# A decoder block on one core: a third split buffer in the input projection's seven products, a moved emptying of PSUM banks, a delayed multiply in the last norm

## The chip, the core and the metric

The kernel runs on one core of a Trainium2 chip. Its engines work side by side and wait for each other through semaphores: TensorE (PE in the profile, with its weight loads as PEld), VectorE (DVE), ScalarE (ACT), GpSimd (POOL) and SyncE (SP, which here issues the DMAs of the weights). The metric is the device time of one execution in microseconds, as the median of several runs. The chip's profiler also recorded one execution; from that record come the profile page and every view quoted here.

## What is computed

One layer for 256 positions of a model of width 2048, everything in float32:

```python
x = x + 0.5 * swiglu_ffn(rms_norm(x, ffn1_norm), w_gate1, w_up1, w_down1)   # d_ff = 5632
z = rms_norm(x, mix_norm) @ w_in                                           # 2048 -> 5 * 1024
lru_x, lru_gate, sc_b, sc_c, sc_x = split(z, 5)
xc = causal_depthwise_conv(lru_x, lru_conv_w) + lru_conv_b
y_lru = rg_lru(xc, ...) * gelu(lru_gate)
y_sc = sc_b * causal_depthwise_conv(sc_c * sc_x, sc_conv_w)
y = concat([rms_norm(y_lru, lru_out_norm), rms_norm(y_sc, sc_out_norm)])
x = x + y @ w_out
x = x + 0.5 * swiglu_ffn(rms_norm(x, ffn2_norm), w_gate2, w_up2, w_down2)
return rms_norm(x, final_norm)
```

The stages are called ffn1, the mixer (with the input projection `w_in`), the output projection, ffn2 and the final norm in what follows. In the code `D` is 2048, `S` is 256 positions, `NT` is 2 (tiles of 128 positions), `CW` is 512 (columns of one block), `UK` is 4 (rows of 128 in one unit).

## The kernel before

**Units of weight.** All weights pass through as units of 512 rows by 512 columns (1 MB, one DMA on SP's queue into the pool `raws`, or a larger buffer). Float32 accuracy comes from splitting: ACT casts a unit to a rounded high part (two casts of 128x1024), DVE subtracts it from the raw unit to get the low part (one operation of 128x2048), and PE multiplies high by high, high by low of the activations, and low by high. That is `parts_of` (L207) with `split_tiles` (L193) and `low_part` (L202). In a trace a unit is a pair `hi_...`, `lo_...`; a unit used for one target has 8 matmuls with the high part and 4 with the low part, each 128x512.

**Where the high and low parts lie.** `split_tiles` takes them from the pool `splits`, which has two buffers of each. While the list `extra` is not empty, every call counts `turn_of["split"]` up, and each third call takes its pair from the pool `extra[0]` instead, where that pair has one buffer. Both ffn stages put their own pool in `extra` (L523) and empty it at their end; the output projection does so with the pool `op` (L1250). Nothing resets the count. Pools on the same side of the memory that are opened one after the other use the same bytes: the pool of ffn2 is opened where `op` has been closed.

**The seven products.** `seven` (L411) multiplies two blocks of rows and columns with seven products in place of eight: p0, p4, p5, p6, p2, p3 and p1 on sums and differences of raw units made by DVE (rows `raw_x<-raw_x,raw_x`), and between them the units x01, x11, x00, x10, which are used as they are. Its banks of PSUM are called a, c, e and d; after p0 and p4 their contents are put aside as the snapshots s1 and s5 (later u2 and u3), and the bank is used again. A function `between`, if it is given, is called at fixed places: `between(0)` after s5, `between(1)` after x01, and so on. Ffn1 and ffn2 run `seven` for gate, up and down projections; the input projection runs it once, as in_c, inside `sc_c`; the output projection as o_q.

**The input projection.** `columns` (L332) computes four banks of 128 columns by 256 positions over four units. The first call (in_0_0) is followed by `use(ps, half)`, which is `lru_x` there: it empties the four banks with two copies by ACT and two adds and multiplies by DVE for each pair (rows `half_x` and `zx`), and then `sc_c()` runs the seven products in_c. The next call of `columns` is in_0_1.

**The output projection.** `product` o0 in two halves (g0, g1) inside the mixer, then, with the pool `op`, `product` o3 in two halves (units o3_0_0, o3_0_1, o3_1_2, o3_1_3) and the seven products o_q with their snapshots in `op`. The results are added into `xres`, the residual (rows `xres<-ps_...`, and `xres<-s_o_q` for the snapshot s1, the last of all). The norm for ffn2 needs squares of `xres` (`junk_n`) and its transposes (`pt_n`).

**Ffn2 and the end.** Ffn2 begins with the units g2_0_0, u2_0_0, g2_0_1, u2_0_1 and so on. Its last down projection is a `product` d2_9_0, the seven products d2_9, and a `product` d2_9_3. Each finished block c of 512 columns of `xres` goes through `last(c, t)` (L1302): a square with its sum on ACT, and on DVE a multiply of `xres` by -0.5 and by the final gain `fin`. `close` then scales the rows and writes them out.

**Who orders the work.** SP's DMAs keep the order of the program. For the other engines a scheduler orders the instructions when the kernel is built, from its own estimates of times and the dependences between tiles; on the chip each engine then runs its own list strictly in that order.

Of the kernel before, what the change touches and what calls it, by code (L numbers as in the profile page):

```python
# [49 lines left out]
def hybrid_block(ctx: ExitStack, tc: tile.TileContext, a: dict, out: bass.AP):  # L50
# [121 lines left out]
    def big(name):  # L172

        return bigs.tile([P, UK, 2 * S], F32R, tag="big", name=name)
# [4 lines left out]
    turn_of = {"split": 0}  # L179

    def load(src, name, pieces=((0, UK),), loaded=None, kept=False):
        if kept and extra:
            raw = extra[0].tile([P, UK, CW], F32, tag="kept", name=f"raw_{name}", bufs=2)
        elif kept:
            raw = bigs.tile([P, UK, CW], F32, tag="big", name=f"raw_{name}")
        else:
            raw = raws.tile([P, UK, CW], F32, tag="raw", name=f"raw_{name}")
        for i, e in pieces:
            sp.dma_start(raw[:, i:e, :], src[i * P : e * P].rearrange("(j p) c -> p j c", p=P))
            if loaded:  # L190
                loaded(i)
        return raw

    def split_tiles(name):
        pool, bufs = splits, 2
        if extra:
            turn_of["split"] += 1
            if turn_of["split"] % 3 == 0:
                pool, bufs = extra[0], 1
        return [pool.tile([P, UK, CW], F32R, tag=part, name=f"{part}_{name}", bufs=bufs) for part in ("hi", "lo")]  # L200

# [319 lines left out]
    def ffn(tag, norm, after, opening=False):  # L521
        with tc.tile_pool(name=f"ffn{tag}", bufs=1, side="left") as fp:
# [26 lines left out]
            def settle():  # L549
                while waiting:  # L550
                    turn_hidden(*waiting.pop(0))
# [312 lines left out]
            for s in range(5):  # L864
                cs = (CW + 2 * s * CW, 2 * CW + 2 * s * CW)
                sg = {}

                def total(ps, tiles):
                    for p in tiles[1:]:
                        dve.tensor_tensor(tiles[0], tiles[0], p, op=ALU.add)  # L870
                    if not tiles:
                        return ps
                    dve.tensor_tensor(tiles[0], ps, tiles[0], op=ALU.add)
                    return tiles[0]

                def gate(t, n, ps, tiles):
                    g = total(ps, tiles)
                    sg[t, n] = tiles[0] if tiles else keep(f"z{tag}_{s}")
                    act.activation(sg[t, n], g, AF.Silu)

                def up(t, n, ps, tiles):
                    dve.tensor_tensor(sg[t, n], total(ps, tiles), sg[t, n], op=ALU.mult)
                    if (t, n) == (1, 0):
                        settle()
                    waiting.append((1 + 2 * s + n, t, sg[t, n], s % 2 == 0))

                def meanwhile(i):
                    if opening and s == 0:
                        two, last, high, low = left[0]
                        if i == "first sum":  # L890
                            two()
                        elif i == "second product":
                            for k in (5, 6):
                                high(k)
                                low(k)
                        elif i == "third sum":
                            last()
                            high(2)
                        elif i == "third low":
                            low(2)  # L900
                        elif i == "fifth product":
                            Engine.pinned = False
                        elif i == "sixth product":
                            first_hidden()
                    elif i == 1:
                        settle()
                    elif s == 0 and i == 0:
                        sums()

                seven(wg, (0, 1), cs, sf, xs, f"g{tag}_{s}", keep, gate, meanwhile, opening and s == 0)  # L910
                sp.held = False
                seven(
                    wu, (0, 1), cs, sf, xs, f"u{tag}_{s}", keep, up,
                    (lambda i: settle() if i == 1 else None) if opening and s == 0 else None,
                )
                if s % 2 == 0:
                    down(s == 4)
# [49 lines left out]
    with tc.tile_pool(name="mixer", bufs=1, side="left") as mp, tc.tile_pool(name="mixw", bufs=2, side="left") as mw:  # L967
# [168 lines left out]
            last()  # L1136
            part(2)

        def sc_c():
            r2 = work.tile([P, NT], F32, tag="r2", name="r2")  # L1140
            dve.tensor_tensor(r2, nm.r, nm.r, op=ALU.mult)
            rt = [r2[:, t : t + 1] for t in range(NT)]
            room = [tmp(tag, "snap", 4 * S, bufs=1) for tag in "vd"]
            free = [b[:, o : o + CW] for b in room for o in (0, CW)]
            z = {}

            def turn(n):
                for f in range(0, 4, 2):
                    pt = bank(f"pt_c{n}_{f}")
                    for i in range(2):  # L1150
                        for t in range(NT):
                            o = i * S + t * P
                            pe.transpose(pt[:, o : o + P], z[t, n][:, (f + i) * P : (f + i + 1) * P], ident)
                    for i in range(2):
                        q = 4 * (1 - n) + f + i
                        c = tmp("cc", q, S + 2, bufs=8)
                        nc.gpsimd.memset(c[:, :2], 0.0)
                        act.copy(c[:, 2:], pt[:, i * S : (i + 1) * S])
                        cc[q] = c

            def done(t, n, ps, tiles):
                for p in tiles[1:]:
                    dve.tensor_tensor(tiles[0], tiles[0], p, op=ALU.add)
                    free.append(p)
                if tiles:
                    z[t, n] = tiles[0]
                    dve.scalar_tensor_tensor(z[t, n], ps, rt[t], z[t, n], op0=ALU.mult, op1=ALU.add)
                else:
                    z[t, n] = free.pop()
                    act.activation(z[t, n], ps, AF.Copy, scale=rt[t])  # L1170
                if (t, n) == (1, 0):
                    turn(1)

            c0 = 3 * (D // 2)
            seven(
                w_in, (0, 1), (c0 + CW, c0), si, [(u, nm.xT[u]) for u in (2, 3)], "in_c", lambda name: free.pop(0), done,
                factor={"s1": rt[0], "s5": rt[1], "u2": rt[0], "u3": rt[1]},
            )
            return lambda: turn(0)

        def sc_x(ps, half):
# [25 lines left out]
        for i, (use, part, half) in enumerate(order):  # L1207
            ps = columns(w_in, part * (D // 2) + half * CW, nm.xT, f"in_{part}_{half}", behind)
            behind = None
            if i == 0:  # L1210
                flush()
                nm.factor()
                nm.diagonals()
                nm.rows()
                bc = nm.bc
                use(ps, half)
                behind = sc_c()
                gate_weights("a", a["lru_w_a"][0])
                gate_weights("i", a["lru_w_i"][0])
                yT += [big(f"yT_{u}") for u in range(KD // UK)]  # L1220
            else:
                use(ps, half)
# [76 lines left out]

    fss = const.tile([P, NT, NC_D], F32, name="fss")  # L1300
    ov = out.rearrange("(t p) d -> p t d", p=P)

    def last(c, t):
        if c == 0 and t == 0:
            held["fin"] = bigs.tile([P, D], F32, tag="big", name="fin")
            nc.scalar.dma_start(held["fin"], a["final_norm"].partition_broadcast(P))
        fin = held["fin"]
        cs = slice(c * CW, (c + 1) * CW)
        xr = xres[:, t, cs]
        part = fss[:, t, c : c + 1]  # L1310
        junk = work.tile([P, CW], F32, tag="junk", name=f"junk_f_{c}_{t}", bufs=1)
        act.activation(junk, xr, AF.Square, accum_out=part)

        def single(tag):
            return work.tile([P, 1], F32, tag=tag, name=f"{tag}_{t}")


        dve.scalar_tensor_tensor(xr, xr, -0.5, fin[:, cs], op0=ALU.mult, op1=ALU.mult)
        if c == NC_D - 2:
            pre = held[t] = single("pre")  # L1320
            dve.reduce_sum(pre, fss[:, t, : c + 1], axis=AX.X)
            dve.tensor_scalar(pre, pre, 1.0 / D, EPS, op0=ALU.mult, op1=ALU.add)
            if t == 0:
                lastgain = fin[:, D - CW :]
                dve.tensor_scalar(lastgain, lastgain, -0.5, None, op0=ALU.mult)
            act.activation(single("root"), pre, AF.Sqrt)
# [66 lines left out]
```

## Time and profile before

| | us |
|---|---|
| median of 3 runs (lowest to highest) | 1729.67 (1729.08 to 1730.92) |
| profiled execution, its own time | 1729.74 |
| its span in the profile | 1728.0 |
| PE busy | 1716.6 |
| DVE busy | 1509.8 |
| ACT busy | 1077.7 |

How to read it: times in a timeline are microseconds from the start of the span. A row `947.87 0.16 DVE L43 COPY tot_y<-pst 128x2 f32<-128x2 f32 x1 [0.33 <-PE pst L43]` says that one copy (x1) from `pst` to `tot_y` began at 947.87 and took 0.16 us, and that DVE had stood still for 0.33 us before it, until PE had written `pst`. All operations pass through one helper, so they carry the same line, L43, and are told apart by the names of their tiles; numbers and indices at the end of a name are left out (`hi_in_c_p` is the high part of any of p0 to p6, `x8` at the end counts the operations of the group). Matmuls overlap, so the step from one group's start to the next group's start is a better measure of what a group takes than its own duration. A view of windows gives for each engine the busy time and, in brackets, the number of instructions, then the granted clock of PE, the share of the DMA engines and GB/s.

### The profile page before, as it was taken

How to read it: one execution, taken by the hardware profiler on the slowest of the kernel's cores; microseconds unless marked ns; L12 is line 12 of the kernel's file. 1: busy time of each engine (PE TensorE's matmuls, PEld its weight loads, DVE VectorE, ACT ScalarE, POOL GpSimd, SP SyncE). 2: the span in 40 equal slices, each digit the busy share in tenths (PEclk: the TensorE clock that was granted, in tenths of full speed). 3: DMA queues.
4: the chain of work that ended last, by engine and by line, in shares of the span. 5: the costliest groups of instructions: out<-in, count | busy, mean ns of one | idle time of the engine just before them, and what ended most of it. 6: DMA issues, size and time to landing. Idle time of an engine off the chain costs nothing.

```text
span 1728.0 us, 20332 instructions
## 1 busy us (share of the span) xinstructions
PE 1716.6 (99%) x7985; PEld 1433.5 (83%) x7985; DVE 1509.8 (87%) x1239; ACT 1077.7 (62%) x1406; POOL 7.0 (0%) x34
## 2 busy tenths in 40 slices
PE   9999999999999999999999999999999999999998
PEld 8888888888888888878888888888888888888886
DVE  7998989899789898787897989889899887899896
ACT  7666566656466666667966657656556664656654
POOL 0100000000000000000000000000000000000000
PEclk9999999999999999999999999999999999999999
DMA  8564565666466556555566574675665646555743
GB/s 300 191 237 141 208 228 186 206 230 219 156 211 204 202 178 219 171 169 197 172 195 203 188 243 144 199 240 187 212 210 195 218 147 219 195 195 195 257 156 122
DMA packets 174223, 343.22 MB, mean 199 GB/s; under 512 B 5684, under 2 KB 8624, under 8 KB 174000
## 3 DMA queue, kind: packets, MB, share of 16 engines
q1 hardware_dynamic: 173632, 340.81, 58.5%
q8 instruction: 62, 1.02, 0.2%
q10 hardware_dynamic: 176, 1.06, 0.2%
q14 instruction: 33, 0.27, 0.0%
q0 software_dynamic: 320, 0.07, 0.0%
HBM read 339.82 MB, written 2.10 MB: 198 GB/s over the span
## 4 chain that ended last, share of the span: by engine, by line
PE 97%; DVE 1%; DMA 1%; issue 0%; ACT 0%; DVEq 0%; ACTq 0%
PE ps_d L43 13%; PE ps_in L43 10%; PE ps_u_a L43 9%; PE ps_g_a L43 9%; PE ps_g_c L43 6%; PE ps_u_c L43 6%; PE ps_d_a L43 5%; PE ps_u_d L43 5%; PE ps_g_d L43 4%; PE ps_u_e L43 3%; PE ps_d_c L43 3%; PE ps_g_e L43 3%; PE ps_g L43 3%; PE ps_o L43 3%; PE ps_u L43 3%; PE ps_d_d L43 3%
## 5 line engine op out<-in xcount | busy, mean ns | idle before, releaser
L43 ACT CAST hi_g_p<-raw_g 128x1024 fp32r<-128x1024 f32 (+1 forms) x139 | 142.6, 1057 | 102.9 <-DVE raw_g L43 32.6
L43 DVE TENSOR_TENSOR lo_g_p<-raw_g,hi_g_p 128x2048 fp32r<-128x2048 f32 x70 | 159.7, 2287 | 32.0 <-ACT hi_g_p L43 31.8
L43 ACT CAST hi_u_p<-raw_u 128x1024 fp32r<-128x1024 f32 x140 | 141.4, 1050 | 67.6 <-DVE raw_u L43 24.7
L43 DVE TENSOR_TENSOR lo_u_p<-raw_u,hi_u_p 128x2048 fp32r<-128x2048 f32 x70 | 159.2, 2286 | 19.7 <-ACT hi_u_p L43 19.4
L43 PE MATMUL ps_d<-hi_d,h 128*128 128x512 f32 x696 | 166.1, 390 | 0.0
L43 PEld LDWEIGHTS ps_d<-hi_d,h 128*128 128x128 f32 x696 | 130.0, 188 | 26.7
L43 ACT CAST hi_d<-raw_d 128x1024 fp32r<-128x1024 f32 x88 | 88.6, 1048 | 71.6 <-PE ps_u_d L43 17.4
L43 DVE TENSOR_TENSOR lo_d<-raw_d,hi_d 128x2048 fp32r<-128x2048 f32 x44 | 100.6, 2290 | 31.8 <-ACT hi_d L43 31.8
L43 PE MATMUL ps_in<-xT_nm,hi_in 128*128 128x512 f32 x512 | 122.5, 391 | 0.0
L43 ACT CAST hi_d_p<-raw_d 128x1024 fp32r<-128x1024 f32 x84 | 85.1, 1050 | 59.3 <-DVE raw_d L43 40.2
L43 PEld LDWEIGHTS ps_in<-xT_nm,hi_in 128*128 128x128 f32 x512 | 94.0, 188 | 18.9 <-ACT tha L43 0.5
L43 ACT CAST hi_g_x<-raw_g 128x1024 fp32r<-128x1024 f32 (+1 forms) x79 | 81.5, 1059 | 41.7 <-PE ps_g_c L43 24.6
L43 ACT CAST hi_u_x<-raw_u 128x1024 fp32r<-128x1024 f32 x80 | 80.4, 1046 | 38.7 <-PE ps_u_c L43 22.1
L43 DVE TENSOR_TENSOR lo_d_p<-raw_d,hi_d_p 128x2048 fp32r<-128x2048 f32 x42 | 95.6, 2287 | 7.9 <-ACT hi_d_p L43 7.7
L43 DVE TENSOR_TENSOR raw_u<-raw_u,raw_u 128x2048 f32<-128x2048 f32 x40 | 91.6, 2290 | 10.9 <-DMA raw_u<-in_ffn_w_up_dram 10.2
L43 DVE TENSOR_TENSOR lo_g_x<-raw_g,hi_g_x 128x2048 fp32r<-128x2048 f32 x40 | 91.4, 2286 | 7.7 <-ACT hi_g_x L43 7.6
L43 DVE TENSOR_TENSOR lo_in<-raw_in,hi_in 128x2048 fp32r<-128x2048 f32 x32 | 73.3, 2289 | 25.3 <-ACT hi_in L43 25.2
L43 DVE TENSOR_TENSOR raw_g<-raw_g,raw_g 128x2048 f32<-128x2048 f32 x40 | 91.5, 2288 | 4.2 <-DMA raw_g<-in_ffn_w_gate_dram 3.7
L43 DVE TENSOR_TENSOR lo_u_x<-raw_u,hi_u_x 128x2048 fp32r<-128x2048 f32 x40 | 91.4, 2285 | 0.2 <-ACT hi_u_x L43 0.2
L43 PE MATMUL ps_d<-lo_d,h 128*128 128x512 f32 x348 | 86.2, 389 | 0.0
L43 ACT CAST hi_in<-raw_in 128x1024 fp32r<-128x1024 f32 x64 | 63.9, 1044 | 25.4 <-PE ps_in L43 13.8
L43 PEld LDWEIGHTS ps_d<-lo_d,h 128*128 128x128 f32 x348 | 65.3, 188 | 13.6
(471 smaller groups left out, 3740.9 us busy)
## 6 DMA issues: line engine op xcount, KB each, us to landing
raw_d<-in_ffn_w_down_dram SPq DMA_DIRECT2D x88, 1024.0 KB, 5.1
raw_u<-in_ffn_w_up_dram SPq DMA_DIRECT2D x87, 1024.0 KB, 5.3
raw_g<-in_ffn_w_gate_dram SPq DMA_DIRECT2D x86, 1024.0 KB, 5.3
raw_in<-in_w_in_dram SPq DMA_DIRECT2D x32, 1024.0 KB, 5.1
raw_in_c<-in_w_in_dram SPq DMA_DIRECT2D x8, 1024.0 KB, 5.1
raw_o<-in_w_out_dram SPq DMA_DIRECT2D x8, 1024.0 KB, 5.1
raw_o_q<-in_w_out_dram SPq DMA_DIRECT2D x8, 1024.0 KB, 5.1
xres<-in_x_dram SPq DMA_DIRECT2D x3, 512.0 KB, 10.0
```

The lines of the kernel that those rows point to most:

```text
L43: ins = getattr(self.engine, name)(*args, **kwargs)
```

## The change

It does four things.

1. In `sc_c`, `extra` holds the pool `bigs` (ten large buffers) while in_c runs, and is emptied after it. `split_tiles` then counts in_c's eleven splits, and each third one takes its high and low part as two of the large buffers. `load` is fitted to that: a unit that is to be kept goes to the same pool as before.
2. `sc_c` takes a function `between`. The emptying of the first columns' banks, `use(ps, half)`, is no longer called ahead of `sc_c` but inside it, at `between(1)` of in_c, after the unit x01.
3. In `last`, the multiply by the final gain is put in a list `gains` and done at the next call with c other than 0. For c = 0 (two operations) it comes later; for the others it is done at once, as before.
4. One line gets a space at its end.

```diff
     def load(src, name, pieces=((0, UK),), loaded=None, kept=False):
-        if kept and extra:
+        if kept and extra[0] is not bigs:
             raw = extra[0].tile([P, UK, CW], F32, tag="kept", name=f"raw_{name}", bufs=2)
...
             turn_of["split"] += 1
             if turn_of["split"] % 3 == 0:
+                if extra[0] is bigs:
+                    return [big(f"{part}_{name}") for part in ("hi", "lo")]
                 pool, bufs = extra[0], 1
...
-        def sc_c():
+        def sc_c(between):
...
             c0 = 3 * (D // 2)
+            extra.append(bigs)
             seven(
                 w_in, (0, 1), (c0 + CW, c0), si, [(u, nm.xT[u]) for u in (2, 3)], "in_c", lambda name: free.pop(0), done,
+                lambda i: between() if i == 1 else None,
                 factor={"s1": rt[0], "s5": rt[1], "u2": rt[0], "u3": rt[1]},
             )
+            extra.clear()
             return lambda: turn(0)
...
-                use(ps, half)
-                behind = sc_c()
+                behind = sc_c(lambda: use(ps, half))
...
+    gains = []
 
     def last(c, t):
...
-        dve.scalar_tensor_tensor(xr, xr, -0.5, fin[:, cs], op0=ALU.mult, op1=ALU.mult)
+        gains.append(lambda: dve.scalar_tensor_tensor(xr, xr, -0.5, fin[:, cs], op0=ALU.mult, op1=ALU.mult))
+        if c:
+            while gains:
+                gains.pop(0)()
```

## The prediction

> **What bounds the kernel now.** I read the page's first part, then its chain of work that ended last, then the waits of TensorE (PE), and only after these the timeline around each place that the change touches.
>
> ```profile
> span 1728.0 us, 20332 instructions
> ...
> PE 1716.6 (99%) x7985; PEld 1433.5 (83%) x7985; DVE 1509.8 (87%) x1239; ACT 1077.7 (62%) x1406; POOL 7.0 (0%) x34
> ...
> PE 97%; DVE 1%; DMA 1%; issue 0%; ACT 0%; DVEq 0%; ACTq 0%
> ```
>
> PE is busy for 1716.6 of 1728.0 us and is 97% of the chain: whatever doesn't make PE wait longer or less costs nothing. The profiled execution took 1729.74 us by its own time, 1.7 us beside the span and 0.07 above the median of the runs (1729.67), so sums made on it stand for the median. The waits say how little can be won:
>
> ```profile
> engine line waited for: us in total, times, longest us
> PE idle L43 <- DVE ones L43: 1.1, 1, 1.1
> PE ps_in_c_c L43 <- ACT v_snap L43: 0.8, 1, 0.8
> PE ps_u_c L43 <- DVE lo_u_p L43: 0.8, 1, 0.8
> PE ps_d_a L43 <- DVE lo_d_p L43: 0.3, 1, 0.3
> ```
>
> The first wait is the start of the run, the third stands in ffn1; the change touches neither. The second (the seven products named in_c) and the fourth (the last ones, in ffn2's last down projection) are its two targets.
>
> **In_c: the moved adds and the third buffer.** The block's opening in the timelines of PE, VectorE (DVE) and ScalarE (ACT), whose columns are start, time, engine, operation, count, and in brackets the wait before:
>
> ```profile
> 732.20 1.07 PE L43 MATMUL ps_in_c_a<-lo_in_c_p,xT_nm 128*128 128x512 f32 x4
> 733.11 1.98 PE L43 MATMUL ps_in_c_c<-hi_in_c_p,xis 128*128 128x512 f32 x8
> 734.92 1.98 PE L43 MATMUL ps_in_c_e<-hi_in_c_x,xT_nm 128*128 128x512 f32 x8
> 736.87 1.21 PE L43 MATMUL ps_in_c_c<-lo_in_c_p,xis 128*128 128x512 f32 x4
> 738.87 2.10 PE L43 MATMUL ps_in_c_c<-hi_in_c_x,xT_nm 128*128 128x512 f32 x8 [0.78 <-ACT v_snap L43]
> 731.87 0.75 DVE L43 TENSOR_TENSOR half_x<-ps_in,half_x 128x256 f32<-128x256 f32 x2
> 733.87 0.75 DVE L43 TENSOR_TENSOR zx<-half_x,bc_nm 128x256 f32<-128x256 f32 x2
> 734.53 2.28 DVE L43 TENSOR_TENSOR lo_in_c_p<-raw_in_c,hi_in_c_p 128x2048 fp32r<-128x2048 f32 x1
> 738.12 0.69 ACT L43 ACTIVATE v_snap<-ps_in_c_c,r 128x512 f32<-128x512 f32 x1 [1.62 <-PE ps_in_c_c L43]
> ```
>
> Four matmuls take 0.91 us undisturbed (732.20 to 733.11), eight 1.81 (733.11 to 734.92). From 734.92 on the steps are 1.95 for eight and 2.00 for four: 0.14 and 1.09 too long, 1.23 in all. The cause is readable: eight adds and multiplies of DVE (731.87 to 734.53, 2.66 us) stand ahead of the low part of unit p4, so the four low matmuls wait until 736.87, the snapshot of their bank until 738.12, and the next use of that bank until 738.87. In the order in which the built changed kernel issues DVE's work the eight stand behind that low part. Taking 2.66 from 734.53 gives 731.87; but the low part of x01, now in a buffer of its own, and one more sum have come ahead of it, and it is ready about 734.2 by my count, while PE wants it at 734.92. The bank's snapshot then falls near 736.4, its next use at 737.64: this stall goes. No instruction is added; the eight adds only go later, behind 2.28 us low parts that have about 0.2 us to spare where they are thinnest (the next pair). Against it, at the end of the block:
>
> ```profile
> 772.37 1.99 ACT L43 CAST hi_in<-raw_in 128x1024 fp32r<-128x1024 f32 x2 [0.61 <-DMA raw_in<-in_w_in_dram]
> 773.56 2.71 PE L43 MATMUL ps_in<-xT_nm,hi_in 128*128 128x512 f32 x11
> ```
>
> The next columns' first cast waits for its DMA, and PE starts 0.15 us after the first half of that cast (772.37 + 1.0 = 773.4). A PE that is 1.23 us earlier would stand there unless the load, issued by SP behind a buffer that DVE frees, also comes earlier; by the order it does, nearly as much. I give back some 0.1. In_c: **-1.1**, bounds -1.23 and -0.5.
>
> **The phase of the count.** The change also does something that it doesn't name. `turn_of["split"]` is one count for the whole kernel, and in_c now adds its 11 splits to it. 11 leaves 2 over 3, so from the output projection on, other units are the third ones. In the outs, unit o3_0_0 and o3_1_3 come from the large pool in place of o3_1_2; and ffn2's very first unit, g2_0_0, comes from the newly opened pool of ffn2, whose memory was the outs' own. Before, that unit took its turn in the ordinary buffers:
>
> ```profile
> 1013.82 2.00 ACT L43 CAST hi_g<-raw_g 128x1024 fp32r<-128x1024 f32 x2 [0.19 <-PE ps_o_q_a L43]
> 1020.84 2.28 DVE L43 TENSOR_TENSOR lo_u<-raw_u,hi_u 128x2048 fp32r<-128x2048 f32 x1
> 1023.03 0.74 DVE L43 SCALAR_TENSOR_TENSOR xres<-ps_o_q_a,r_y,xres 128x512 f32<-128x512 f32 x1
> 1023.70 0.74 DVE L43 SCALAR_TENSOR_TENSOR xres<-ps_o_q_d,r_y,xres 128x512 f32<-128x512 f32 x1
> 1024.47 0.75 DVE L43 SCALAR_TENSOR_TENSOR xres<-s_o_q,r_y,xres 128x512 f32<-128x512 f32 x1
> 1021.78 1.07 PE L43 MATMUL ps_o_q_d<-lo_o_q_p,yT 128*128 128x512 f32 x4
> 1022.69 3.79 PE L43 MATMUL ps_g<-hi_g,xT_n 128*128 128x512 f32 x16
> ```
>
> The cast of g2_0_0 was done at 1015.8, seven us before PE wanted it at 1022.69. Now its tile lies where the outs kept their snapshots, and the last reader of that memory is the add of s1 into xres, the row at 1024.47. The order of the changed kernel puts this wait on ACT's cast, and puts one thing more ahead of the add on DVE: the low part of g2_0_1, which ACT casts first. So: add d ends its turn at 1024.47; the low part takes 2.19 (1020.84 to 1023.03), to 1026.66; the add 0.75, to 1027.41; the first half of the cast 1.0 (half of 2.00), to 1028.4; and some 0.1 to reach PE: 1028.5. PE has nothing else in its order there, g2_0_0 is still its first unit. The wait is 1028.5 - 1022.69 = **+5.8**. Its start is tied to PE (the add of d needs PE's last matmuls), so no earlier gain shortens it. From below: with the add straight behind d, 5.8 - 2.19 = 3.6. From above: the whole cast instead of half, 6.8. Queued behind the waiting cast on ACT are the second half, two squares and the norm's root; the low matmuls of g2_0_0 need DVE to finish that low part, two 0.65 us adds later: near 1031.9, and PE asks after 16 matmuls of 0.227, at 1032.1. Thin, but covered.
>
> In the outs' opening the same shift puts the transposes of the new residual straight behind the first unit:
>
> ```profile
> 959.25 0.16 DVE L43 COPY tot_y<-pst 128x2 f32<-128x2 f32 x1 [1.92 <-PE pst L43]
> 964.58 1.41 DVE L43 SCALAR_TENSOR_TENSOR xres<-ps_o,r_y,xres 128x512 f32<-128x512 f32 x2
> 964.65 1.30 PE L43 MATMUL ps_o<-hi_o,yT 128*128 128x512 f32 x5
> 965.78 0.60 PE L43 MATMUL pt_n<-ident,xres 128*128 128x128 f32 x4
> ```
>
> PE would ask for the two adds at 964.65, not 965.78. On DVE two low parts stood between 959.25 and 964.58; in the new order it is one low part (2.2) and one 0.69 us add, so the adds end near 964.58 - 2.2 + 0.6 + 1.41 = 964.4: in time by 0.2. The other low part has moved into the 1.92 us that DVE waited before 959.25, which just holds it. I take 0, bounds 0 and +0.8.
>
> **The clock behind a 5.8 us wait.** The nearest row to a PE that stood still is the start of the run:
>
> ```profile
> 0.00:6.00 6.00, 4.73 (x20) 4.17 (x20) 0.95 (x4) 2.63 (x5) 0.69 (x6) 1.00 0.63 198
> 1.05 2.93 PE L43 MATMUL idle<-ones 128*128 128x128 f32 x12 [1.05 <-DVE ones L43]
> 4.13 1.11 PE L43 MATMUL pt_n<-ident,xres 128*128 128x128 f32 x4
> 5.89 1.24 PE L43 MATMUL ps_g<-hi_g,xT_n 128*128 128x512 f32 x4 [0.22 <-ACT hi_g L43]
> 7.42 0.60 PE L43 MATMUL pt_n<-ident,xres 128*128 128x128 f32 x4
> ```
>
> The granted clock is given as 1.00 for this stretch (the column ahead of the DMA share), yet four transposes at 4.13 took 1.11 us where four of the same at 7.42 took 0.60. So PE is slow from 1.05 to about 5.89, 4.84 us. At half speed that loses 2.4. Whether 5.8 us of idling suffices to bring this about no row shows: the waits of 0.8 above don't. I bound it by 0 and +2.4 and, as 5.8 us is longer than the whole slow stretch, take the upper end: **+2.4**. The Trainium skill, "TensorE: Matmul & The Clock Gate", Part 1 (the HAM clock gate), says that an idle window of about 3.4 us halves the clock, and that a busy one restores it; the slow start here agrees, and no run here yet shows the falling back. By that page too a gap of 5.8 us would mostly, and one of 3.6 only seldom, contain a whole window, and the loss would be an estimated 1.7 to 3.4.
>
> **The last block.** Two of the eight multiplies of xres by the final gain leave their place:
>
> ```profile
> 1661.74 1.29 DVE L43 SCALAR_TENSOR_TENSOR xres<-xres,fin 128x512 f32<-128x512 f32 x2
> 1667.30 2.29 DVE L43 TENSOR_TENSOR lo_d_p<-raw_d,hi_d_p 128x2048 fp32r<-128x2048 f32 x1 [0.86 <-ACT hi_d_p L43]
> 1668.95 0.39 PE L43 MATMUL ps_d_e<-hi_d_x,h 128*128 128x512 f32 x1
> 1669.64 1.19 PE L43 MATMUL ps_d_a<-lo_d_p,hs 128*128 128x512 f32 x4 [0.30 <-DVE lo_d_p L43]
> ```
>
> One matmul (0.227) fills 1668.95 to 1669.64, so 0.46 is stall, and that is all there is to win. Without the pair DVE is 1.2 us earlier, but the phase again sends the low part of x11 (2.2) and one of the two multiplies (0.6) ahead of that of p5: 1667.30 less the 0.86 it waited, less 1.2, plus 2.8 gives 1668.0, ready at 1670.25. PE, with two matmuls to fill, asks at 1669.4: 0.85 of stall for 0.46. I take **+0.3** (bounds -0.5, +1.0). The other multiply goes behind the low part of p2, where DVE is ahead. The tail after the last matmul keeps its instructions. The space in the third hunk is nothing.
>
> **Sum.** -1.1 + 5.8 + 0 + 2.4 + 0.3 = +7.4; 1729.7 + 7.4 = **1737.1 us**.
>
> **The rivals.** *The clock stays up* through the gap: 7.4 - 2.4 = +5.0, 1734.7. For it: the granted clock's column shows 1.00 even at the start. Against: the slow transposes. *Not slower*: the tile of g2_0_0 comes free without the wait, because the snapshot's last reader on DVE is done by 1021.6 (cast half of 1.0 before 1022.69). That needs the s1 add to be taken 5.8 us earlier than the order has it, ahead of the low parts of u2_0_0 and g2_0_1; from there on the price is nothing and the sum -1.1 + 0.3 = -0.8, 1728.9. Against it: the add of d stands ahead in the same queue and needs PE's matmuls that run until 1022.85 (1021.78 + 1.07). *The change does only what its words say*, both stalls gone and the phase without effect: 1729.7 - 1.2 - 0.5 = 1728.0. *A half gap*, 3.6 with the clock up: 1729.7 - 1.1 + 3.6 + 0.3 = 1732.5.
>
> **How the numbers follow.** Forecast 0.45, the clock up 0.33, a half gap 0.07, not slower 0.07, words only 0.05, and 0.03 for a further wait in the shifted blocks of ffn2. Changes within 0.2% (3.5 us) can't be told from none: slower is above 1733.2, faster below 1726.2. The first two and the last are slower (0.81); the others lie within, but for a small part of each (0.15); nothing listed gets below 1726.2, and I leave 0.04 for it. Range: the lower end takes in the rival with the clock up with a shorter gap, 1731.8; the upper the forecast with the upper bounds of the outs and the last block, 1737.1 + 0.8 + 0.7 = 1738.6, and a full 6.8 us gap, 1739.6. The forecast's own is 1735.5 to 1739.6.
>
> **What would show it.** A wait of 5 to 6 us of ps_g for ACT's hi_g at ffn2's opening, the largest of PE's waits, with the cast itself released by DVE's xres. Behind it, matmuls of 0.45 in place of 0.227 us for 3 to 5 us if the clock falls. No wait of ps_in_c_c for v_snap, the step at 736.87 back to 0.91. A wait of ps_d_a for lo_d_p of 0.6 to 0.9. A span under 1730 with no wait for hi_g would make the prediction wrong at its root; a gap without slow matmuls would leave only its last term wrong.

## The result, and the profile after

| | before | changed | ratio, 95% interval |
|---|---|---|---|
| first comparison, median of 7 and 7 runs | 1729.67 us | 1735.12 us | 1.0032 [1.0020, 1.0043] |
| second comparison (21 and 5 runs) | 1729.99 us | 1736.44 us | 1.0041 [1.0028, 1.0054] |
| profiled execution, its own time | 1729.74 us | 1733.94 us | |

The change makes the kernel slower, by 5.5 and 6.5 us of the medians (the ratios, which are not those of the medians, give 5.5 and 7.1). The changed kernel's profiled execution is the lowest of its seven, so the two traces are 4.2 us apart. The page of the changed kernel, its first part:

```profile
span 1732.2 us, 20321 instructions
...
PE 1716.9 (99%) x7985; PEld 1434.8 (83%) x7985; DVE 1510.4 (87%) x1239; ACT 1076.7 (62%) x1406; POOL 7.0 (0%) x34
```

PE has the same 7985 matmuls and is busy for 0.3 us more, in a span that is 4.2 longer: most of the loss is waiting. (Slow matmuls count as busy; the 1.65 us that they cost, shown below, are nearly hidden in this sum by other groups that became shorter.) The waits of PE name it:

```profile
PE ps_g L43 <- ACT hi_g L43: 6.0, 2, 5.6
PE idle L43 <- DVE ones L43: 1.1, 1, 1.1
```

The two waits that the change was to remove are gone from this trace (v_snap, and lo_d_p in the last block); one that is larger than both has come. The most useful reading is a table of drift: the start of the same matmuls in both traces. What changes between two rows happened between them.

| group of matmuls | before | changed | drift | step |
|---|---|---|---|---|
| ffn1, low part of the second up product | 99.47 | 98.52 | -0.95 | -0.95 |
| in_c, high part of p4 | 733.11 | 732.05 | -1.06 | -0.11 |
| in_c, first low part of x01 | 740.81 | 738.39 | -2.42 | -1.36 |
| in_0_1, first unit | 773.56 | 771.02 | -2.54 | -0.12 |
| output projection, low part of o3_0_0 | 962.83 | 960.28 | -2.55 | 0.0 |
| o_q, low part into bank d | 1021.78 | 1019.20 | -2.58 | 0.0 |
| ffn2, high part of g2_0_0 | 1022.69 | 1025.85 | +3.16 | +5.74 |
| ffn2, low part of g2_0_0 | 1026.31 | 1031.12 | +4.81 | +1.65 |
| last block, high part of p5 | 1667.14 | 1671.79 | +4.65 | -0.16 |
| end of the last matmul | 1719.73 | 1723.94 | +4.21 | -0.44 |

The first step belongs to no edit. Both kernels issue the same there, and in before's trace the low part came late because a sum waited for its DMA:

```profile
94.33 2.29 DVE L43 TENSOR_TENSOR raw_u<-raw_u,raw_u 128x2048 f32<-128x2048 f32 x1 [1.05 <-DMA raw_u<-in_ffn_w_up_dram]
```

In the changed kernel's trace it did not. It is one of the things that differ between executions; the traces of two other kernels hold such a wait too, of 0.4 us each.

In_c, in the timeline of the changed kernel (PE, then DVE):

```profile
732.05 1.98 PE L43 MATMUL ps_in_c_c<-hi_in_c_p,xis 128*128 128x512 f32 x8
733.86 1.07 PE L43 MATMUL ps_in_c_c<-lo_in_c_p,xis 128*128 128x512 f32 x4
734.77 1.98 PE L43 MATMUL ps_in_c_e<-hi_in_c_x,xT_nm 128*128 128x512 f32 x8
736.58 1.98 PE L43 MATMUL ps_in_c_c<-hi_in_c_x,xT_nm 128*128 128x512 f32 x8
738.39 1.07 PE L43 MATMUL ps_in_c_e<-lo_in_c_x,xT_nm 128*128 128x512 f32 x4
...
733.02 0.75 DVE L43 TENSOR_TENSOR half_x<-ps_in,half_x 128x256 f32<-128x256 f32 x2
```

Every step is 0.91 or 1.81 us. The low matmuls of p4 come straight behind its high ones, and the adds that stood ahead of their low part start at 733.02, behind it. From p4's high part to in_0_1 it is 38.97 us here and 40.45 before, 1.48 less.

The opening of ffn2 in the changed kernel (PE, DVE, ACT):

```profile
1019.20 1.07 PE L43 MATMUL ps_o_q_d<-lo_o_q_p,yT 128*128 128x512 f32 x4
1025.85 5.43 PE L43 MATMUL ps_g<-hi_g,xT_n 128*128 128x512 f32 x16 [5.58 <-ACT hi_g L43]
1031.12 1.98 PE L43 MATMUL ps_g<-lo_g,xT_n 128*128 128x512 f32 x8
...
1021.77 2.28 DVE L43 TENSOR_TENSOR lo_g<-raw_g,hi_g 128x2048 fp32r<-128x2048 f32 x1
1023.97 0.75 DVE L43 SCALAR_TENSOR_TENSOR xres<-s_o_q,r_y,xres 128x512 f32<-128x512 f32 x1
...
1024.75 1.99 ACT L43 CAST hi_g<-raw_g 128x1024 fp32r<-128x1024 f32 x2 [3.36 <-DVE xres L43]
```

Read it backwards: PE waits for ACT's cast; the cast waited 3.36 us for DVE's `xres`, the add of the snapshot s1 that ends at 1024.72; and that add stood behind 2.28 us of the next unit's low part. Sixteen matmuls then took 5.27 us (1025.85 to 1031.12) where before they took 3.62 (1022.69 to 1026.31): slow matmuls follow the wait.

### The profile page after: what moved, and what is told of

It is laid out like the page before. It is cut to its first block, busy times and chain, and to the rows that moved or that the text cites. A ratio compares the mean times of both kernels' runs of the same rounds, so it can differ in the third digit from the quotient of the medians.

```text
span 1732.2 us, 20321 instructions
## 1 busy us (share of the span) xinstructions
PE 1716.9 (99%) x7985; PEld 1434.8 (83%) x7985; DVE 1510.4 (87%) x1239; ACT 1076.7 (62%) x1406; POOL 7.0 (0%) x34
## 3 DMA queue, kind: packets, MB, share of 16 engines
q10 hardware_dynamic: 176, 1.06, 0.1%
## 4 chain that ended last, share of the span: by engine, by line
PE 99%; DVE 0%; ACT 0%; issue 0%; DVEq 0%; ACTq 0%
PE ps_d L43 14%; PE ps_in L43 10%; PE ps_g_a L43 9%; PE ps_u_a L43 9%; PE ps_u_c L43 6%; PE ps_g_c L43 6%; PE ps_d_a L43 5%; PE ps_u_d L43 5%; PE ps_g_d L43 5%; PE ps_d_c L43 3%; PE ps_u_e L43 3%; PE ps_g_e L43 3%; PE ps_g L43 3%; PE ps_o L43 3%; PE ps_u L43 3%; PE ps_d_d L43 3%
```

## The experiments

Each experiment was timed beside the kernel before on the same chip, and profiled once.

**1. The phase of the count.** Four kernels ask whether the loss is the shifted count, and what in it makes PE wait. The first takes the shift back behind in_c:

```diff
             extra.clear()
+            turn_of["split"] -= 11
             return lambda: turn(0)
```

> The changed kernel, with 11 taken off the count of splits behind in_c, so that the output projection and ffn2 have the phase of the kernel before. Theory (the whole loss is the phase: the first unit of ffn2 lands on the snapshots' memory): no wait of ps_g for hi_g over 0.3 us, matmuls behind it at full rate; time 1727.9 (before, less 1.3 of in_c, less up to 0.5 of the last block). Rival (the loss comes from the moved adds or the large buffers of in_c themselves): still 1734 or more.

Measured: 1728.53 us, 0.9988 [0.9979, 0.9996] of before (1730.43). The wait is gone, and the kernel is now faster than before. The second puts nothing but the shift into the kernel before:

```diff
+            turn_of["split"] += 11
             return lambda: turn(0)
```

> The kernel before, with nothing but 11 added to the count of splits behind in_c. Theory: the same wait of ps_g for hi_g, 5.5 to 6 us, and 1.5 us of slow matmuls behind it; time 1729.7 + 7.3 = 1737.0, slower than the changed kernel by the in_c stall that stays. Rival: within 1 us of before.

Measured: 1739.16 us, 1.0046 [1.0032, 1.0060], 8.7 us above before by the medians and 8.0 by the ratio. Its waits of PE:

```profile
PE ps_g L43 <- ACT hi_g L43: 6.1, 2, 5.6
PE ps_d_a L43 <- DVE lo_d_p L43: 1.2, 1, 1.2
PE idle L43 <- DVE ones L43: 1.1, 1, 1.1
PE ps_in_c_c L43 <- ACT v_snap L43: 0.8, 1, 0.8
```

One added number, no other edit, and the same 5.6 us wait. What lies beyond the expected difference of 7.3 is partly in the last block, where the stall is 1.40 in place of 0.47 (experiment 4), and partly in the slow matmuls, which cost 1.98 us for the expected 1.5 (sixteen took 5.60, not 3.62). The third sets the count to zero where ffn2 begins, so that only the output projection stays shifted:

```diff
             extra.append(fp)
+            turn_of["split"] = 0
```

> The changed kernel with the count set to 0 at the start of each ffn stage (it is 0 at ffn1's anyway): the output projection keeps the shifted phase, ffn2 has that of before. Theory: the wait at ffn2's opening is gone and the outs cost nothing; time 1727.9, like the full restoration. Rival (the shifted phase costs something within the output projection too): some 0.5 to 1 above the full restoration.

Measured: 1727.55 us, 0.9983 [0.9975, 0.9992]. The shift within the output projection costs nothing. The fourth keeps the whole shift, but lets the snapshots be added ahead of the bank:

```diff
-            add(2 - n, t, 0, *([] if ps is None else [ps]), *tiles)
+            add(2 - n, t, 0, *tiles, *([] if ps is None else [ps]))
```

> The changed kernel with its shifted phase, but the snapshots of o_q are added into xres ahead of the bank they belong to, so that the last reader of the snapshots' memory is no longer the last add. Theory (PE waits because that add is late, not because the tile lies in the other pool): the cast of g2_0_0 runs before PE is done with the output projection, no wait over 0.5 us; time 1727.5 to 1728.5. Rival (the other pool's tile is late for another reason, such as its one buffer or its load): the wait of 5 us stays, 1734 or more.

Measured: 1728.91 us, 0.9987 [0.9979, 0.9996]. In its timeline (DVE, ACT, PE):

```profile
1019.22 0.75 DVE L43 SCALAR_TENSOR_TENSOR xres<-s_o_q,r_y,xres 128x512 f32<-128x512 f32 x1
...
1020.00 3.90 ACT L43 CAST hi_g<-raw_g 128x1024 fp32r<-128x1024 f32 x4 [0.48 <-DVE xres L43]
...
1020.95 1.07 PE L43 MATMUL ps_o_q_d<-lo_o_q_p,yT 128*128 128x512 f32 x4
1021.86 3.79 PE L43 MATMUL ps_g<-hi_g,xT_n 128*128 128x512 f32 x16
```

The cast still waits for that add, but the add ends at 1019.97, and the cast's first half is done before PE asks at 1021.86. So neither the other pool nor its single buffer is what costs: it is that the memory's last reader stood last in DVE's queue.

**2. The slow matmuls.** 26 matmuls of ones, as 52 passes of 0.11 us, fill the wait:

```diff
+                for _ in range(26):
+                    pe.matmul(ps["g", 0][:, :P], ones, ones, start=True, stop=True)
                 for u in range(KD // UK):
```

> The changed kernel with 26 matmuls of ones on PE ahead of ffn2's first unit, into the bank that this unit then begins anew, so that PE works while it waits for the cast (52 passes of 0.11 us, 5.7 us, just the length of the wait). The wait itself stays as long. Theory (the seven slow matmuls behind the wait are PE's clock, lowered by its idling): they run at 0.227 us, time 1735.1 - 1.6 = 1733.5. Rival (they are slow for another reason, such as ACT's second cast or DVE reading the same memory): still 0.43 us each, 1735.1 or more.

Measured: 1735.51 us, 1.0025 [1.0015, 1.0035]. PE in its timeline:

```profile
1021.83 5.97 PE L43 MATMUL ps_g<-ones 128*128 128x128 f32 x52
1027.56 3.97 PE L43 MATMUL ps_g<-hi_g,xT_n 128*128 128x512 f32 x16
1031.37 1.98 PE L43 MATMUL ps_g<-lo_g,xT_n 128*128 128x512 f32 x8
```

The unit begins 5.73 us behind the end of the projection, as in the changed kernel, its sixteen matmuls take 3.81 us, not 5.27, and the granted clock is 1.00 from 1020 to 1031, while ACT's second cast runs as it did. The slow matmuls are a consequence of PE's idling. It is the trace that shows this. The time of 1733.5 was missed: 1735.51 is 4.9 us above the kernel before beside it (1730.60), and 1.0025 stands against 1.0032 and 1.0041 of the changed kernel, with intervals that overlap. The trace of this run holds 0.9 us of waiting for a load at the start, 0.4 us in ffn1 and a stall of 1.05 us in the last block, which the changed kernel's first trace doesn't have. Then half as many, so that PE idles for the second half only, and beside it the changed kernel once more:

```diff
-                for _ in range(26):
+                for _ in range(13):
```

> The changed kernel with 13 matmuls of ones at the beginning of the wait ahead of ffn2 (2.85 us), so that PE idles for 2.9 us of the 5.7. If the clock falls only after an idling longer than that, the matmuls behind run at 0.227 us and the time is 1.5 us below the changed kernel of the same call (1734.0). If 2.9 us of idling suffice, they take 0.43 us again and the time is that of the changed kernel.

> The changed kernel once more, beside the next ones on the same chip. The last block's stall (0.11 us in the first trace) was 1.05 us in another kernel that issues the same there; if it hangs on when the 1 MB of the final gain lands, as the traces so far suggest, it differs from the first trace here too. Time 1735 to 1736.

Measured: 1735.43 us, 1.0038 [1.0026, 1.0051], beside 1736.44, 1.0041 [1.0028, 1.0054], which is a little above the 1735 to 1736 expected. PE in the timeline of the kernel with 13:

```profile
1022.36 3.07 PE L43 MATMUL ps_g<-ones 128*128 128x128 f32 x26
1028.09 5.31 PE L43 MATMUL ps_g<-hi_g,xT_n 128*128 128x512 f32 x16 [2.67 <-ACT hi_g L43]
1033.24 1.98 PE L43 MATMUL ps_g<-lo_g,xT_n 128*128 128x512 f32 x8
```

5.15 us for sixteen, and a granted clock of 0.50 (last section): here 2.9 us of idling lowered the clock as 5.7 did.

**3. In_c by its parts.** Only the move of the first columns' emptying, in the kernel before:

```diff
-        def sc_c():
+        def sc_c(between):
...
+                lambda i: between() if i == 1 else None,
...
-                use(ps, half)
-                behind = sc_c()
+                behind = sc_c(lambda: use(ps, half))
```

> The kernel before with only the emptying of the first columns' banks moved into in_c. Theory (the eight adds ahead of p4's low part made the stall): 1.3 us of it goes, 1728.4. Rival (without a third buffer the low parts still queue for the two): a stall of 0.5 or more stays at another place of in_c.

Measured: 1731.56 us, 1.0007 [0.9999, 1.0016] of before (1730.60). Its waits of PE hold two new ones:

```profile
PE ps_in_c_a L43 <- ACT hi_in_c_p L43: 1.0, 1, 1.0
PE ps_in L43 <- ACT hi_in L43: 0.9, 1, 0.9
```

The old stall is gone, but another stands in its place, as the rival had it. DVE begins the sum for p5 here:

```profile
739.88 2.28 DVE L43 TENSOR_TENSOR raw_in_c<-raw_in_c,raw_in_c 128x2048 f32<-128x2048 f32 x1
```

That is 5.84 us behind the start of p4's high part, as in the kernel before (5.83), since the same adds and low parts stand ahead of it; PE comes to p5 earlier and waits 0.98. In the changed kernel the low part of x01 is made ahead of all this (at 720.43, and at 720.39 in the kernel with the buffer alone, which follows), and the sum begins 3.63 us behind the start of p4's high part. The second wait is for the next columns' load. It was issued no later, counted from p4's high part (33.31 us, before 33.43), but landed 7.08 us after its issue, where the four other traces with that order of in_c show 5.83 to 6.62; whether the move had a part in that stays open. The move by itself is worth nothing, or a little less. Only the third buffer (with `load` fitted as in the change), and the count restored behind it:

```diff
+                if extra[0] is bigs:
+                    return [big(f"{part}_{name}") for part in ("hi", "lo")]
...
+            extra.append(bigs)
             seven(
...
+            extra.clear()
+            turn_of["split"] -= 11
```

> The kernel before with only the third split buffer of in_c, the count restored behind it. Theory: the eight adds stay ahead of p4's low part, the stall of about 1.3 us in in_c stays, 1729.7. Rival: the buffer alone lets the scheduler put the low part first, 1728.4.

Measured: 1729.00 us, 0.9991 [0.9982, 0.9999]. The wait that remains in in_c:

```profile
PE ps_in_c_c L43 <- ACT v_snap L43: 0.3, 1, 0.3
```

By the time, 1.6 us below the 1730.60 beside it, this is nearer to the rival, but not by the rival's mechanism. The eight adds still stand ahead of p4's low part:

```profile
733.44 2.28 DVE L43 TENSOR_TENSOR lo_in_c_p<-raw_in_c,hi_in_c_p 128x2048 fp32r<-128x2048 f32 x1
```

It begins 1.43 us behind the start of p4's high part, before 1.42. What has changed is that the low part of x01 is ready by then, so that PE has two of its matmuls to do in the gap; 0.49 us of stall are left. The length of in_c sums it up, from p4's high part to in_0_1: 40.45 us in the kernel before, 41.49 with the move alone (0.93 of it the wait for the load), 39.59 with the buffer alone, and 38.97 or 38.98 in all eight traces that have both. The move takes away what the buffer leaves, once the buffer is there.

**4. The last block.** Only the delayed multiply, in the kernel before:

```diff
+    gains = []
...
-        dve.scalar_tensor_tensor(xr, xr, -0.5, fin[:, cs], op0=ALU.mult, op1=ALU.mult)
+        gains.append(lambda: dve.scalar_tensor_tensor(xr, xr, -0.5, fin[:, cs], op0=ALU.mult, op1=ALU.mult))
+        if c:
+            while gains:
+                gains.pop(0)()
```

> The kernel before with only the multiply of the last norm delayed. Theory (the delay frees DVE ahead of p5's low part): the stall of 0.57 us in the last block is gone, 1729.2. Rival (it went with the phase, which changed the order of the low parts): the stall stays, 1729.7.

Measured: 1730.68 us, 1.0002 [0.9993, 1.0011]; no wait of lo_d_p in its trace. Equal in time, then, and yet the stall was gone; and kernels that issue the same instructions in the last block had different stalls. The second trace of the changed kernel shows what varies (DVE, then PE):

```profile
1653.51 0.43 DVE L43 TENSOR_SCALAR fin<-fin 128x512 f32<-128x512 f32 x1 [2.87 <-DMA fin<-in_final_norm_dram]
...
1675.08 0.61 PE L43 MATMUL ps_d_e<-hi_d_x,h 128*128 128x512 f32 x2
1677.14 1.20 PE L43 MATMUL ps_d_a<-lo_d_p,hs 128*128 128x512 f32 x4 [1.44 <-DVE lo_d_p L43]
```

The same three rows in its first trace:

```profile
1650.38 0.43 DVE L43 TENSOR_SCALAR fin<-fin 128x512 f32<-128x512 f32 x1 [1.22 <-DMA fin<-in_final_norm_dram]
...
1673.60 0.61 PE L43 MATMUL ps_d_e<-hi_d_x,h 128*128 128x512 f32 x2
1674.08 1.20 PE L43 MATMUL ps_d_a<-lo_d_p,hs 128*128 128x512 f32 x4
```

A small operation of `last`, the scaling of the last block's gain by -0.5, stands in DVE's queue ahead of the last block's low parts and waits for the 1 MB of `fin` to land. With 1.22 us of that wait PE has no stall some 23 us later, with 2.87 it has 1.60. DVE comes to this row 22.63 us ahead of p5's high part in both traces; what moved is the landing, 5.6 and 7.3 us after the load's issue. Over all traces that have this row, with the stall as the step into the low matmuls less 0.23 us for each matmul in it:

| order of the last block | DVE's wait for fin : PE's stall, us |
|---|---|
| kernel before (also the move alone, the buffer alone) | 1.80 : 0.13, 2.12 : 0.47, 2.90 : 1.07 |
| delayed multiply, phase of before | 2.33 : 0, 2.63 : 0.23, 2.81 : 0.40 |
| changed kernel's (delayed multiply, shifted phase) | 1.22 : 0.03, 1.94 : 0.68, 2.31 : 1.05, 2.78 : 1.51, 2.87 : 1.60 |
| shifted phase, no delay | 2.98 : 1.40 |

In each row with several pairs the stall follows the wait nearly one for one; it is the wait less some 1.7, 2.4 and 1.3 us, and 1.6 in the single trace of the last row. So the delayed multiply is worth 0.7 us of lateness in the phase of before, and the shift turns that into a loss of 0.4. From issue to landing the load took 5.6 to 7.4 us in these twelve traces. Two kernels take the wait itself away, by folding the scaling into `close`, where DVE has time:

```diff
-            if t == 0:
-                lastgain = fin[:, D - CW :]
-                dve.tensor_scalar(lastgain, lastgain, -0.5, None, op0=ALU.mult)
...
-        dve.tensor_tensor(y3[:, h * w : (h + 1) * w], xres[:, t, o], fin[:, o], op=ALU.mult)
+        dve.scalar_tensor_tensor(y3[:, h * w : (h + 1) * w], xres[:, t, o], -0.5, fin[:, o], op0=ALU.mult, op1=ALU.mult)
```

> The kernel before with only that scaling folded into close. Theory: the stall of 0.57 us in the last block goes, 0.5 below before, no DVE wait for the gain's DMA of over 0.3 us ahead of p0's low part. Rival (the two multiplies at c = 0 make the stall): it stays at 0.5.

Measured: 1729.68 us, 1.0002 [0.9993, 1.0011]; no wait for lo_d_p in its trace, and no stall in the last block. The 0.5 us expected of it can't be seen in the time. And together with the reset of the count in the changed kernel:

> The changed kernel with the count set to 0 at the start of each ffn stage, and with the scaling of the last block's gain by -0.5 folded into the multiply of close, so that no DVE instruction waits for the gain's DMA ahead of the last block's low parts. Theory (that wait makes the last block's stall, 0 to 1.3 us from run to run): no wait of ps_d_a for lo_d_p, 1727.0, 0.3 to 0.7 below the reset alone. Rival (the stall comes from the multiplies themselves): as the reset alone, 1727.6, with a stall of 0.2 to 0.5 left.

Measured: 1727.88 us, 0.9986 [0.9977, 0.9995]. All the waits of PE that its profile lists:

```profile
PE idle L43 <- DVE ones L43: 1.1, 1, 1.1
PE ps_g L43 <- ACT hi_g L43: 0.2, 1, 0.2
```

Nothing is left but the start of the run. Its trace has the shortest span of all (1724.9 us), but its median can't be told from the reset alone (0.9983): some 0.5 us is below what these runs resolve, and the traces alone show it. Both are faster than the kernel before beside them, by 2 to 3 us with intervals that leave out 1.

## Why the prediction was right, and which term was off

The forecast was 1737.1 us, slower; measured 1735.12, and 1736.44 later.

- *In_c, -1.1.* The drift shows -1.36, and -1.48 up to the next columns, which is outside the bounds of -1.23 and -0.5. The mechanism was as told, but the count of the stall ended too early: the eight matmuls behind it took 1.94 us for 1.81 (738.87 to 740.81). The 0.1 given back for the next load was not needed either: that load was issued 30.40 us behind p4's high part, before 33.43, so that it had 3 us more to land. That the move needs the buffer to be a gain at all was not seen.
- *The first unit of ffn2, +5.8.* 5.74 in both traces, in the place, by the chain and behind the very low part named. The rivals without a gap, or with half of one, fall. Their mechanism was real, though: with the add of s1 in time (the fourth kernel) there is no wait at all.
- *The outs, 0.* 0.0; the adds that the transposes need ended in time, and the shift without ffn2's part of it cost nothing.
- *The clock, +2.4.* This was the term that was mis-sized. The slow stretch is shorter than at the start of the run: the 5.27 us for 16 matmuls are 1.65 more than 3.62. Three other traces lost 1.5, 1.5 and 2.0 us there. The step that failed was to price the slow stretch by the whole slow start, 4.84 us: the clock was down for 6.83 us here, but 3.6 of these lay inside the wait itself, and only 3.2 us of work were slow (1025.85 to 1029.09). Half of that is the 1.6 lost. Its reason, that 5.8 us is longer than the slow start, was none either, since a gap of 2.9 is enough. The mechanism itself is shown by the filled wait, and the rival "the clock stays up" falls. The rival of a half gap had counted on the clock staying up at 3.6 us; the kernel with 13 filling matmuls speaks against that too.
- *The last block, +0.3.* The first trace shows -0.44, the second a stall of 1.60 where 0.47 was. Both are the landing of `fin`. At an equal landing, the changed order is later by 0.4 (thresholds of 1.3 and 1.7), which is what the prediction worked out; what it took for fixed from its one trace, when DVE comes to the last block's low parts, is not. The 2.12 us that DVE had waited for a DMA in that trace, 20 us earlier, it left out. So +0.3 can't be checked by any one run, and where a run falls between -0.4 and +1.1 is chance.

At equal landings the terms sum to -1.5 + 5.7 + 1.6 + 0.4 = +6.2 us, by the side of +5.5 and +6.5 measured. The forecast of +7.4 was 1.2 above that sum, by 0.8 for the clock and 0.4 for in_c.

## What to carry to other kernels

A count or rotation that outlives its stage couples stages: whoever adds uses in one place moves the choice in all later ones, so reset it where a stage begins, or compare the order of the whole program and not of the edited block. When a pool is opened on memory that another has just left, ask for the last reader of that memory and where it stands in its engine's queue: one add of 0.75 us, last in its queue, held PE for 5.7. And before a stall of a microsecond is credited to an edit, look for a DMA in the chain behind it: here one landing varied by 1.8 us.

## What the runs showed of the hardware

The clock's fall and return can be read from the granted clock in narrow windows (the last column but two). The changed kernel, its second trace, and the kernel with 13 filling matmuls:

```profile
1022.00:1022.50 0.50, 0.00 (x0) 0.00 (x0) 0.50 (x1) 0.00 (x0) 0.00 (x0) 0.76 0.81 135
1022.50:1029.00 6.50, 3.15 (x7) 2.48 (x8) 5.74 (x6) 3.34 (x6) 0.00 (x0) 0.50 0.97 331
1029.00:1029.50 0.50, 0.50 (x3) 0.42 (x2) 0.31 (x3) 0.12 (x1) 0.00 (x0) 0.91 1.05 410
```

```profile
1026.50:1027.00 0.50, 0.00 (x0) 0.00 (x0) 0.50 (x1) 0.50 (x1) 0.00 (x0) 0.94 0.61 143
1030.00:1030.50 0.50, 0.50 (x3) 0.39 (x2) 0.50 (x1) 0.00 (x0) 0.00 (x0) 0.65 1.05 406
```

```profile
1027.50:1028.00 0.50, 0.00 (x0) 0.00 (x0) 0.50 (x2) 0.50 (x2) 0.00 (x0) 0.70 1.04 143
1031.00:1031.50 0.50, 0.50 (x4) 0.41 (x3) 0.47 (x3) 0.00 (x0) 0.00 (x0) 0.89 1.05 410
```

A window of 0.5 us at 0.76 was at full rate for 0.26 and at half for 0.24. So the clock fell at 1022.26, 1026.94 and 1027.70, and returned at 1029.09, 1030.35 and 1031.11: after 6.83, 3.41 and 3.41 us, one step or two. In the kernel before with the shift alone it fell at 1027.70 and returned at 1034.52 (0.70 and 0.98 in the windows from 1027.50 and from 1034.50): two steps again. In the three views PE had idled for 2.15 (from 1020.11), 5.17 (from 1021.77) and 2.49 us (from 1025.21) when it fell. The best reading is that the changes come on a grid of 3.41 us that takes no notice of the kernel, and that a gap costs more or less by where it lies on it. A step need not be idle throughout: the clock fell when PE had been idle for only 2.15 us. In the second trace the step before the one that lowered the clock, if the grid holds there, had 1.76 us of idling and did not lower it; nor did the 1.60 us stall of the last block. The Trainium skill, "TensorE: Matmul & The Clock Gate", Part 1 (the HAM clock gate), describes such a free-running window of 3413 ns, and asks for a whole idle one; the traces agree with its length, and not with the whole.

The slow start of the run isn't equally long in all traces either, though the granted clock is 1.00 throughout there. In before's trace the four matmuls begun at 5.89 took 1.07 us to the next group; in that of the kernel with the phase restored, the same four begun at the same time took 1.87:

```profile
5.89 2.08 PE L43 MATMUL ps_g<-hi_g,xT_n 128*128 128x512 f32 x4 [0.22 <-ACT hi_g L43]
7.76 1.05 PE L43 MATMUL ps_g<-lo_g,xT_n 128*128 128x512 f32 x2
```

The first up projection begins at 13.93 there, before at 11.97, 1.96 us later with the same instructions. The two traces of the changed kernel differ in the same place by 1.76 us (11.94 and 13.70), which with the landing of `fin` (1.57) makes up the 3.0 us between their spans, less 0.3 elsewhere. That this start ends on the grid too would fit, but isn't shown. Together with the late load in ffn1 (0.95) such differences come to 4.5 us; runs of the kernel before spread over 6 (1728 to 1734), and the two small edits of this change could win less than 2.
